# Stick-breaking attention scores: the low part of k held per head in both partition halves, and the second score product run over 128 rows

## The chip, the cores and the metric

The kernel runs on one core of a Trainium2 chip. The metric is the device time of one execution in microseconds (us). The program has five instruction streams: TensorE (PE in the profile; its weight loads are listed apart as PEld), VectorE (DVE), ScalarE (ACT), GpSimd (POOL) and the queue that issues DMAs (SP).

## What is computed

One hybrid decoder layer over x of 1024 tokens by 1024 channels: one input projection; three causal mixers of 256 channels each (stick-breaking attention, HGRN2, GLA); a sigmoid-gated merge of their up-projections; an output projection; residual and layer norm. The change lies in the stick-breaking mixer, which has 4 heads of 64 channels:

```python
z = einsum('bhtd,bhsd->bhts', q, k) * 64 ** -0.5        # per head, s < t
log_beta, log_one_minus = log_sigmoid(z), log_sigmoid(-z)
tail = reverse_cumsum(log_one_minus, over s) - log_one_minus
weights = exp(log_beta + tail)                          # 0 where s >= t
out = einsum('bhts,bhsd->bhtd', weights, v)
```

Inputs and output are float32.

## The kernel before

Matrix products run in a 32-bit matmul type (F32R). To keep accuracy, an operand is split into a high part (a cast) and a low part (the operand minus its cast), and a product is the sum of high·high, low·high and high·low. The helper `split` (lines 97 to 99) does that for weights, for x and for attention weights: the cast is ScalarE's (L98), the subtraction VectorE's (L99).

**Projections.** x^T lies in SBUF in two parts. `proj_T` (L207) makes 128 channels by 512 tokens with 24 matmuls of 512 columns; `proj_N` (L220) makes 128 tokens by 256 or 272 channels with 24 matmuls. They are written as generators that form one stream, in a fixed order: v, then q and k of unit 0, of unit 1, the gates, GLA's inputs, and so on.

**Chains.** The mixers are generators too (`c_sb` for stick-breaking, `c_rec` for the recurrences). The program walks through a chain and, at each `yield`, puts some matmuls of the stream into it, as many as a budget allows. The order on each engine is set when the program is built, by a scheduler that goes by priorities and by which buffers are free; on the chip each engine works through its list in that order.

**Scores.** A unit is two heads, 128 channels. `f_qk` projects k and q of a unit in two halves of 512 tokens. Heads are kept apart by partition half: rA is partitions 0 to 63, rB is 64 to 127. For head 0, `q0` has the high part of q in rA and its low part in rB, and `k0` has the high part of k in both halves; so one product over 128 rows is (high q + low q)·(high k). For head 1 it is the same with the halves changed over (`q1`, `k1`). The low part of k is one tile `l` for both heads: head 0 in rA, head 1 in rB. The second product of a score (L559) therefore takes one half only, 64 rows.

`c_sb` works through 24 chunks per unit, each of 128 queries and up to 512 keys of one head. `weights` makes the score z with two matmuls (L558, L559) into one of two PSUM tiles, two sigmoids on ScalarE (L560, L561), a select on GpSimd where the chunk holds the diagonal (L565), and on VectorE a scan (L569) and a product (L570). Three chunks later `transposed` turns the result with up to four matmuls (L585) and splits it into `ath` (ScalarE, L98) and `atl` (VectorE, L99). One chunk after that `values` multiplies them with v (L607).

**Buffers.** Tiles made by `H` come from one pool of 29 buffers of 128 x 512 x 4 bytes (`NHALF`): 8 of v, the tiles of q and k, the chain's outputs `oT`, and much else.

Of the kernel before, what the change touches and what calls it, by code (L numbers as in the profile page):

```python
# [7 lines left out]
F32 = mybir.dt.float32  # L8
F32R = mybir.dt.float32r
# [3 lines left out]
ALU = mybir.AluOpType  # L13
# [4 lines left out]
T = 1024  # L18
# [37 lines left out]
def hybrid_layer_kernel(ctx, tc, x, x_t, w_in, gla_gate_w2, gla_gate_b, hgrn_lb_logits,  # L56
# [44 lines left out]
    def split3(parts, src):  # L101
        """three parts of bf16 that sum up to src; src is overwritten"""
        nc.scalar.copy(parts[0], src)
        nc.vector.tensor_tensor(src, src, parts[0], op=ALU.subtract)
        nc.scalar.copy(parts[1], src)
        nc.vector.tensor_tensor(parts[2], src, parts[1], op=ALU.subtract)

    def parts3():
        """room for three parts of two halves"""
        a, b, c = [H("prod", BF16, [P, 2, 512]) for _ in range(3)]  # L110
        return [(t[:, 0], t[:, 1], c[:, th]) for th, t in enumerate((a, b))]

    def pairs(pr1, Q, K):
        """products of the odd queries and the keys before them, at the places of these keys"""
        t_ = GT("prod")[:, 0:256]
        nc.vector.tensor_tensor(t_, Q[:, 1::2], K[:, 0::2], op=ALU.mult)
        for p_ in pr1:
            nc.gpsimd.memset(p_[:, 1::2], 0.0)
        split3([p_[:, 0::2] for p_ in pr1], t_)

    class at_priority:
        """trace order within a class; the class of the lower number goes first on an engine"""
        stack, seq = [0], 0
# [18 lines left out]

# [1 line left out]
    wz = const.tile([P, 512], BF16, name="wz")  # L144
# [20 lines left out]

# [1 line left out]
    def load_w(src, c0, width=256, extra=None, between=None):  # L167
        """src [(k p), c], columns c0..c0+width: per k the two parts of the weights [p, width]."""
        nk = src.shape[0] // P
        n = min(nk, 512 // min(width, 256))  # L170
        ks = []
        wt = width if extra is None else width + 16
        for u in range(nk // n):
            raw = wp.tile([P, n, wt], F32, tag="wr", name=nm("wr"), bufs=NWR)
            rows = src[u * n * P:(u + 1) * n * P]
            nc.sync.dma_start(raw[:, :, 0:width], rows[:, c0:c0 + width].rearrange("(k p) c -> p k c", p=P))
            if extra is not None:
                nc.sync.dma_start(raw[:, :, width:wt], rows[:, extra:extra + 16].rearrange("(k p) c -> p k c", p=P))
            wh = wp.tile([P, n, wt], F32R, tag="wh", name=nm("wh"), bufs=5)
            wl = wp.tile([P, n, wt], F32R, tag="wl", name=nm("wl"), bufs=5)  # L180
            with at_priority(PW):
                split(wh, wl, raw)
            ks += [(wh[:, k], wl[:, k]) for k in range(n)]
            if between is not None and u == 1:
                between()
        return ks

# [1 line left out]
    xh = [[xp.tile([P, 4, 512], F32R, tag="x", name=nm("xh")) for _ in range(2)] for _ in range(2)]  # L189
# [10 lines left out]
    def proj_T(ws, th):  # L200
        """generator; the product is what it returns"""
        pt = pmm()
        n = 0
        for k, (wh, wl) in enumerate(ws):
            a, b = xh[th][k // 4][:, k % 4, :], xl[th][k // 4][:, k % 4, :]
            for w_, x_ in ((wh, a), (wh, b), (wl, a)):
                mm(pt, w_, x_, start=(n == 0), stop=(n == 23))  # L207
                n += 1
                if n % 6 == 0 and n < 24:
                    yield 1.3  # L210
        return pt
# [13 lines left out]

# [1 line left out]
    # rows of three products: high high, high low, low high  # L227
    w2 = const.tile([16, P], F32, name="w2")
# [19 lines left out]

    # lower bound of HGRN2: softmax over the depth axis (one layer), cumulated, minus its first row
    lb = const.tile([P, 2], F32, name="lb")  # L250
# [14 lines left out]

    # ======== the stream of projections: generators that yield the time of the tensor engine ========
    def f_av():
# [12 lines left out]
    def f_qk(un):  # L280
        uk = load_w(W, A_K + un * P, P)
        ks, qs, kl = ([], []), ([], []), []
        for th in range(2):
            pt = yield from proj_T(uk, th)
            k0, k1, l = H("ks", F32R), H("ks", F32R), H("kl", F32R)
            nc.scalar.copy(k0[rA], pt[rA])
            nc.scalar.copy(k0[rB], pt[rA])
            nc.scalar.copy(k1[rB], pt[rB])
            nc.scalar.copy(k1[rA], pt[rB])
            nc.vector.tensor_tensor(l[rA], pt[rA], k0.bitcast(F32)[rA], op=ALU.subtract)  # L290
            nc.vector.tensor_tensor(l[rB], pt[rB], k1.bitcast(F32)[rB], op=ALU.subtract)
            ks[0].append(k0)
            ks[1].append(k1)
            kl.append(l)
            yield 1.3
# [35 lines left out]
    def f_cv():  # L331
# [35 lines left out]
        def decay():  # L367
            # f = exp(log_sigmoid(x) / 16), log_sigmoid(x) = min(x, 0) - log(1 + exp(-|x|))
            lower_bound()
# [41 lines left out]
    def f_h(un):  # L411
        uf = load_w(W, H_F + un * P, P)
        f, K, Q = [], [], []
        for th in range(2):
# [3 lines left out]
            nc.scalar.activation(s2, pt, AF.Sigmoid, scale=-1.0)  # L418
            # f = sigmoid(z) (1 + lb exp(min(-z, 60))) = sigmoid(z) + lb min(sigmoid(-z), e^60 sigmoid(z))
            nc.vector.scalar_tensor_tensor(e, s1, E60, s2, op0=ALU.mult, op1=ALU.min)  # L420
# [18 lines left out]
    def f_finish(c0, gain, key, out_key):  # L439
        """gate of a recurrence in natural layout, then y^T."""  # L440
        ws = load_w(W, c0)
# [90 lines left out]

    # ======== chains: generators that yield (time of the chain, share of the tensor engine) ========
    def c_sb(un):
# [11 lines left out]
        def weights(c):  # L546
            """z, beta and 1 - beta, products from the right: the weights of 128 queries and up to 512 keys"""
            hd, jp, g, ti = c
            hr = (rA, rB)[hd]
            i = jp * 2 + ti  # L550
# [7 lines left out]
            mm(pt[:, 0:cm], qq[:, th], ks[hd][g][:, 0:cm], start=True, stop=False)  # L558
            mm(pt[:, 0:cm], qq[hr, th], kl[g][hr, 0:cm], start=False, stop=True)  # L559
            nc.scalar.activation(om[:, 0:cw], pt[:, 0:cw], AF.Sigmoid, scale=-0.125)  # L560
            nc.scalar.activation(be[:, 0:cw], pt[:, 0:cw], AF.Sigmoid, scale=0.125)  # L561
            if last:
                # keys before the query: 1 - beta = 1 and beta = 0 elsewhere
                for a_, fill in ((om, 1.0), (be, 0.0)):
# [11 lines left out]
        def transposed(c):  # L576
# [11 lines left out]
            if ni < ns:  # L588
                # block above the diagonal
                for a_ in (ath, atl):  # L590
                    nc.vector.tensor_scalar(a_[:, ni, ts], ident, 0.0, None, op0=ALU.mult)
# [39 lines left out]
    def c_rec(key, nh, V):  # L631
        """windows of 128; G decay, K key [k, t], Q query; V [t, v]; two halves of t side by side."""
        G, K, Q, pr = d[key]
# [13 lines left out]
        sc = [S("sc", shape=[P, wpb, nh, P]) for _ in range(nbank)]  # L647
        # block-diagonal queries, the odd blocks of a level
        parts = nh == 4
# [3 lines left out]
        if parts:  # L653
            # products of two exact parts; the low parts of the queries by two windows
            Qlo = [[R("Qlo", F32R, [P, nh, P]) for _ in range(2)] for _ in range(2)]
# [50 lines left out]
        for h in LEVELS:  # L706
            nb = 64 // h
            for hf in range(2):
# [11 lines left out]
                yield R4_T if nh == 4 else R2_T  # L720
        # keys in rows of t
        kn = []
# [6 lines left out]
        yield RK_T  # L729
        # states at the starts of windows 1..7, block-diagonal over heads  # L730
        spt = 512 // ncol
# [8 lines left out]
        for b in range(nbank):  # L740
# [13 lines left out]
            yield RS_T / nbank  # L754
        # o = q S + scores v, RMS norm per head
        wpt = 512 // ncol
# [27 lines left out]

    # ======== interleaving: chains first, the stream of projections in their gaps ========
    stream = [("V", f_av()), (("qk", 0), f_qk(0)), (("qk", 1), f_qk(1)), (("ag", 0), f_ag(0)),
# [9 lines left out]
    def advance():  # L796
        """one step of the stream; its time on the tensor engine, or None when it is at its end"""
        while pos[0] < len(stream):
# [53 lines left out]

# [1 line left out]
    wout(range(NWO, 8))  # L854
# [3 lines left out]
    for tq in range(4):  # L858
# [4 lines left out]
        for t2 in range(2):  # L863
# [38 lines left out]
            else:  # L902
                # some of the columns go through ScalarE and GpSimd
                ca, cb, cc = slice(0, 192), slice(192, 640), slice(640, D)
# [41 lines left out]
```

## Time and profile before

| | |
|---|---|
| median of 3 runs | 847.0 us (846.96 to 847.02) |
| the profiled execution: its span, which is also its time | 847.0 us |
| PE busy | 98% of the span, 4576 matmuls |
| PE weight loads busy | 82% |
| DVE busy | 59% |
| ACT busy | 42% |
| POOL busy | 16% |
| DMA, mean over the span | 55 GB/s |
| the first score product starts at | 55.7 us |
| the last score product of `c_sb` starts at | 214.4 us |

"Busy" counts the time in which an engine has an instruction running. Matmuls overlap each other in TensorE's pipeline and their ends are modelled, so 98% does not mean that the engine works at its peak: the distance from the start of one matmul to the start of the next says what a matmul costs. Of an engine other than PE the busy time can be taken as it stands.

### The profile page before, as it was taken

To read this page: it belongs to the slowest core of one execution; us is meant where nothing else is said; L and a number is where in the kernel's file an instruction comes from. 1 tells how busy PE (TensorE), PEld (TensorE's weight loads), DVE (VectorE), ACT (ScalarE), POOL (GpSimd) and SP (SyncE) were. 2 spreads that over 40 slices of the span, in tenths; PEclk is the share of its full clock that TensorE was granted. 3 is DMA by queue.
4 is the path that set the end of the run, shared out by engine and by line. 5 is a ranking of instruction groups with operands and counts; after the bars stand their busy time and mean duration, and the time that the engine had idled before them with its cause. 6 is when DMAs were issued, how large, how long until landed. Compare 5 with 4: busy or idle time off the path is not lost.

```text
span 847.0 us, 12334 instructions
## 1 busy us (share of the span) xinstructions
PE 830.7 (98%) x4576; PEld 697.8 (82%) x4576; DVE 496.7 (59%) x1025; ACT 353.2 (42%) x733; POOL 138.9 (16%) x234
## 2 busy tenths in 40 slices
PE   8999999999999999999999999999999999999996
PEld 7977788777778989988888889888888888878886
DVE  6449886868999868687754124221233223256665
ACT  6457564686634636454655123221222222241110
POOL 3011212022310011422210002222222121110000
PEclk9999999999999999999999999999999999999998
DMA  9421010110011111020412120221212122132211
GB/s 266 108 53 26 26 26 1 45 26 21 24 38 39 40 37 26 2 62 20 126 37 81 38 69 16 54 57 38 57 38 61 32 63 63 44 125 100 95 54 50
DMA packets 66508, 46.22 MB, mean 55 GB/s; under 512 B 4353, under 2 KB 61329, under 8 KB 66449
## 3 DMA queue, kind: packets, MB, share of 16 engines
q1 hardware_dynamic: 65008, 42.36, 18.1%
q10 hardware_dynamic: 1440, 3.08, 1.0%
q8 instruction: 36, 0.59, 0.3%
q14 instruction: 24, 0.19, 0.1%
HBM read 41.23 MB, written 4.19 MB: 54 GB/s over the span
## 4 chain that ended last, share of the span: by engine, by line
PE 88%; DVE 8%; issue 1%; DMA 1%; ACT 0%; POOL 0%; SPq 0%; POOLq 0%; DVEq 0%; ACTq 0%
PE mm L207 43%; PE mm L220 14%; PE mm L878 10%; PE mm L503 7%; PE z L693 4%; PE z L559 2%; PE av L607 2%; PE tr L585 2%; PE av L766 2%; DVE Qlo L677 1%; PE z L558 1%; PE av L764 1%; DVE om L569 1%; DMA wr<-in_w_out_dram 1%; PE z L744 1%
## 5 line engine op out<-in xcount | busy, mean ns | idle before, releaser
L207 PE MATMUL mm<-xh,wh 128*128 128x512 f32 x576 | 233.2, 405 | 0.0
L207 PE MATMUL mm<-xh,wl 128*128 128x512 f32 x576 | 229.2, 398 | 0.0
L207 PE MATMUL mm<-xl,wh 128*128 128x512 f32 x576 | 228.1, 396 | 0.0
L207 PEld LDWEIGHTS mm<-xh,wh 128*128 128x128 f32 x576 | 109.7, 190 | 26.8 <-issue 3.5
L207 PEld LDWEIGHTS mm<-xh,wl 128*128 128x128 f32 x576 | 108.5, 188 | 24.1
L207 PEld LDWEIGHTS mm<-xl,wh 128*128 128x128 f32 x576 | 108.8, 189 | 22.2
L99 DVE TENSOR_TENSOR wl<-wr,wh 128x512 fp32r<-128x512 f32 (+2 forms) x116 | 74.6, 648 | 83.8 <-ACT wh L98 82.8
L98 ACT CAST wh<-wr 128x512 fp32r<-128x512 f32 (+2 forms) x116 | 66.4, 576 | 106.9 <-PE mm L207 92.8
L220 PE MATMUL mm<-wh,xh 128*128 128x256 f32 (+1 forms) x320 | 93.2, 291 | 0.8 <-ACT wh L98 0.8
L220 PE MATMUL mm<-wl,xh 128*128 128x256 f32 (+1 forms) x320 | 91.5, 286 | 0.4 <-DVE wl L99 0.4
L220 PE MATMUL mm<-wh,xl 128*128 128x256 f32 (+1 forms) x320 | 91.0, 285 | 0.0
L878 PE MATMUL mm<-wo,mh 128*128 128x512 f32 (+1 forms) x288 | 80.8, 366 | 0.3 <-DVE wo L99 0.3
L509 POOL TENSOR_TENSOR mT<-mT,gt 128x512 f32<-128x512 f32 x32 | 46.8, 1462 | 179.3 <-DVE gt L508 179.3
L508 DVE TENSOR_TENSOR gt<-mm,gt 128x512 f32<-128x512 f32 x32 | 22.1, 690 | 83.3 <-PE mm L503 83.0
L497 ACT ACTIVATE gt<-mm 128x512 f32<-128x512 f32 x48 | 28.6, 595 | 97.8 <-PE mm L207 91.8
L220 PEld LDWEIGHTS mm<-wh,xh 128*128 128x128 f32 x320 | 61.0, 191 | 2.9 <-ACT wh L98 1.7
L220 PEld LDWEIGHTS mm<-wl,xh 128*128 128x128 f32 x320 | 61.0, 190 | 1.1 <-DVE wl L99 1.1
L220 PEld LDWEIGHTS mm<-wh,xl 128*128 128x128 f32 x320 | 61.0, 191 | 0.1
L878 PEld LDWEIGHTS mm<-wo,mh 128*128 128x128 f32 x288 | 52.0, 189 | 9.5 <-DVE wo L99 0.7
L878 PE MATMUL mm<-wo,ml 128*128 128x512 f32 (+1 forms) x144 | 52.6, 365 | 0.0
L503 PE MATMUL mm<-yl,wh 128*128 128x512 f32 x96 | 38.5, 401 | 1.9 <-DVE yl L99 1.9
L503 PE MATMUL mm<-yh,wl 128*128 128x512 f32 x96 | 38.4, 399 | 0.0
(204 smaller groups left out, 1290.8 us busy)
## 6 DMA issues: line engine op xcount, KB each, us to landing
wr<-in_w_in_dram SPq DMA_DIRECT2D x92, 256.0 KB, 2.9
xraw<-in_x_t_dram SPq DMA_DIRECT2D x16, 256.0 KB, 5.5
xr<-in_x_dram SPq DMA_DIRECT2D x8, 512.0 KB, 3.4
wr<-in_w_out_dram SPq DMA_DIRECT2D x16, 256.0 KB, 2.8
wr<-in_w_up_dram SPq DMA_DIRECT2D x24, 128.0 KB, 2.3
out_dram<-xr SPq DMA_DIRECT2D x7, 256.0 KB, 2.1
out_dram<-xr ACTq DMA_DIRECT2D x7, 256.0 KB, 2.1
lng<-in_ln_g_dram ACTq DMA_DIRECT2D x1, 512.0 KB, 4.8
```

The costliest lines, as they stand in the source:

```text
L98: nc.scalar.copy(hi, src)
L99: nc.vector.tensor_tensor(lo, src, hi.bitcast(F32), op=ALU.subtract)
L207: mm(pt, w_, x_, start=(n == 0), stop=(n == 23))
L220: mm(pt, x_, w_, start=(n == 0), stop=(n == 23))
L497: nc.scalar.activation(gt, pt, AF.Sigmoid)
L503: mm(pu, w_, y_[th], start=(k == 0), stop=(k == 5))
L508: nc.vector.tensor_tensor(gt, pu, gt, op=ALU.mult)
L509: nc.gpsimd.tensor_tensor(mT, mT, gt, op=ALU.add)
L559: mm(pt[:, 0:cm], qq[hr, th], kl[g][hr, 0:cm], start=False, stop=True)
L585: nc.tensor.transpose(pt[:, j, :], be[:, j * P:(j + 1) * P], ident)
L693: mm(pt[:, wi * nh:(wi + 1) * nh], k_[:, w * P:(w + 1) * P], q.rearrange("p a (n h) -> p a n h", h=h), start=(n == 0 and wi == 0), stop=(n ...
L878: mm(pt, l_, r_[e][:, o:o + w], start=(n == 0), stop=(n == 23))
```

## The change

The low part of k is kept per head, each in both partition halves, as the high part is. The second product is then (high q + low q)·(low k) over 128 rows, with the same stationary operand as the first product. It adds the product of the two low parts, which was left out before.

```diff
     def f_qk(un):
         uk = load_w(W, A_K + un * P, P)
-        ks, qs, kl = ([], []), ([], []), []
+        ks, qs, kl = ([], []), ([], []), ([], [])
         for th in range(2):
             pt = yield from proj_T(uk, th)
-            k0, k1, l = H("ks", F32R), H("ks", F32R), H("kl", F32R)
+            k0, k1, l0, l1 = H("ks", F32R), H("ks", F32R), H("kl", F32R), H("kl", F32R)
...
-            nc.vector.tensor_tensor(l[rA], pt[rA], k0.bitcast(F32)[rA], op=ALU.subtract)
-            nc.vector.tensor_tensor(l[rB], pt[rB], k1.bitcast(F32)[rB], op=ALU.subtract)
+            for r_ in (rA, rB):
+                nc.vector.tensor_tensor(l0[r_], pt[rA], k0.bitcast(F32)[rA], op=ALU.subtract)
+                nc.vector.tensor_tensor(l1[r_], pt[rB], k1.bitcast(F32)[rB], op=ALU.subtract)
             ks[0].append(k0)
             ks[1].append(k1)
-            kl.append(l)
+            kl[0].append(l0)
+            kl[1].append(l1)
...
         def weights(c):
             hd, jp, g, ti = c
-            hr = (rA, rB)[hd]
...
             mm(pt[:, 0:cm], qq[:, th], ks[hd][g][:, 0:cm], start=True, stop=False)
-            mm(pt[:, 0:cm], qq[hr, th], kl[g][hr, 0:cm], start=False, stop=True)
+            mm(pt[:, 0:cm], qq[:, th], kl[hd][g][:, 0:cm], start=False, stop=True)
```

Per unit it makes four subtractions more on VectorE and two `H` tiles more. The rest of the diff takes out comments. Line numbers behind the change are up by one or two.

The built order of the instructions moves in a few places while `c_sb` of unit 0 runs. On VectorE, at the first half of unit 1's k: before, the two subtractions L290 and L291 (`kl`) stand ahead of the split of the chain (`atl`) and its scan (`om`).

```order
L591 TENSOR_SCALAR atl_724<-ident 128x128
L290 TENSOR_TENSOR kl_716<-mm_635,ks_714 64x512
L291 TENSOR_TENSOR kl_716<-mm_635,ks_715 64x512
L99 TENSOR_TENSOR atl_724<-tr_725,ath_723 128x128
L569 SCALAR_TENSOR_TENSOR om_739<-om_739 128x128
L99 TENSOR_TENSOR wl_1079<-wr_1076,wh_1078 128x512
L570 TENSOR_TENSOR be_738<-be_738,om_739 128x127
L99 TENSOR_TENSOR atl_724<-tr_751,ath_723 128x2x128
```

With the change (lines 291 and 292):

```order
L592 TENSOR_SCALAR atl_733<-ident 128x128
L291 TENSOR_TENSOR kl_722<-mm_641,ks_720 64x512
L292 TENSOR_TENSOR kl_723<-mm_641,ks_721 64x512
L291 TENSOR_TENSOR kl_722<-mm_641,ks_720 64x512
L99 TENSOR_TENSOR wl_1091<-wr_1088,wh_1090 128x512
L292 TENSOR_TENSOR kl_723<-mm_641,ks_721 64x512
L99 TENSOR_TENSOR atl_733<-tr_734,ath_732 128x128
L570 SCALAR_TENSOR_TENSOR om_748<-om_748 128x128
L99 TENSOR_TENSOR atl_733<-tr_760,ath_732 128x2x128
L571 TENSOR_TENSOR be_747<-be_747,om_748 128x127
```

Four subtractions and the split of a weight (`wl`) now stand ahead of the chain's `atl` and scan. On TensorE some 50 rows of the same stretch are in another order. Before, a chunk's three transposes (`tr_777`) and all products with v (`av_791`) stand ahead of the score z_801:

```order
L585 MATMUL tr_777<-ident,be_682 128x128 x3
L207 MATMUL mm_731<-xh_115,wl_632 128x512
L207 MATMUL mm_731<-xh_115,wh_631 128x512
L207 MATMUL mm_731<-xl_119,wh_631 128x512
L207 MATMUL mm_731<-xh_115,wl_632 128x512
L607 MATMUL av_791<-ath_723,V_205 128x256
L607 MATMUL av_791<-atl_724,V_205 128x256
L607 MATMUL av_791<-ath_723,V_205 128x256
L607 MATMUL av_791<-atl_724,V_205 128x256
L558 MATMUL z_801<-ks_506,qs_617 128x512
L559 MATMUL z_801<-kl_508,qs_617 128x512
```

With the change (the same tiles are tr_786, av_800 and z_810):

```order
L608 MATMUL av_800<-ath_732,V_205 128x256
L559 MATMUL z_810<-ks_506,qs_623 128x512
L560 MATMUL z_810<-kl_508,qs_623 128x512
L207 MATMUL mm_740<-xh_115,wh_637 128x512
L207 MATMUL mm_740<-xl_119,wh_637 128x512
L586 MATMUL tr_786<-ident,be_688 128x128 x3
L207 MATMUL mm_740<-xh_115,wl_638 128x512
L608 MATMUL av_800<-atl_733,V_205 128x256
L608 MATMUL av_800<-ath_732,V_205 128x256
L608 MATMUL av_800<-atl_733,V_205 128x256
```

The transposes and three of the four products with v now stand behind the score and two projection matmuls. By the end of unit 0's first head the two orders agree again on TensorE, and from there on they are the same to the end of the program. ScalarE's list differs in two places by one position; the DMA queue's list is the same.

## Rows read from the trace of the kernel before

**Rows 1.** The page's first part: the span, and the engines' busy time.
```profile
span 847.0 us, 12334 instructions
PE 830.7 (98%) x4576; PEld 697.8 (82%) x4576; DVE 496.7 (59%) x1025; ACT 353.2 (42%) x733; POOL 138.9 (16%) x234
```
**Rows 2.** The chain of work that ended last, by engine.
```profile
PE 88%; DVE 8%; issue 1%; DMA 1%; ACT 0%; POOL 0%; SPq 0%; POOLq 0%; DVEq 0%; ACTq 0%
```
**Rows 3.** Busy time by stretch: length, PE, PEld, DVE, ACT, POOL, clock, DMA.
```profile
50.00:60.00 10.00, 10.00 (x43) 7.46 (x41) 5.16 (x9) 5.37 (x10) 1.11 (x4) 1.00 0.23 56
60.00:90.00 30.00, 29.39 (x137) 21.49 (x137) 26.77 (x50) 21.42 (x46) 5.68 (x12) 1.00 0.08 19
90.00:130.00 40.00, 40.00 (x234) 32.44 (x234) 34.52 (x68) 21.97 (x50) 7.28 (x16) 1.00 0.10 27
130.00:200.00 70.00, 69.33 (x391) 55.50 (x391) 52.56 (x110) 47.21 (x98) 15.74 (x35) 1.00 0.11 27
200.00:220.00 20.00, 19.92 (x100) 14.92 (x99) 19.79 (x36) 13.48 (x30) 2.93 (x8) 1.00 0.10 27
```
**Rows 4.** The same stretches, the 64-row product (L559) alone: PE, PEld.
```profile
50.00:60.00 10.00, 0.77 (x2) 0.36 (x2) 1.00 0.23 56
60.00:90.00 30.00, 5.01 (x11) 2.01 (x11) 1.00 0.08 19
90.00:130.00 40.00, 5.00 (x11) 2.01 (x11) 1.00 0.10 27
130.00:200.00 70.00, 8.31 (x19) 3.47 (x19) 1.00 0.11 27
200.00:220.00 20.00, 2.41 (x5) 0.91 (x5) 1.00 0.10 27
```
**Rows 5.** TensorE in order of time, 512 columns: start us, duration us, instruction.
```profile
82.10 0.39 PE L558 MATMUL z<-ks,qs 128*128 128x512 f32 x1
82.42 0.49 PE L559 MATMUL z<-kl,qs 64*128 64x512 f32 x1
82.84 0.50 PE L207 MATMUL mm<-xh,wh 128*128 128x512 f32 x1
83.18 0.39 PE L207 MATMUL mm<-xl,wh 128*128 128x512 f32 x1
83.41 0.40 PE L207 MATMUL mm<-xh,wl 128*128 128x512 f32 x1
```
**Rows 6.** The weight loads of the same stretch; in brackets idle time before.
```profile
82.42 0.18 PEld L559 LDWEIGHTS z<-kl,qs 64*128 64x128 f32 x1 [0.25 <-issue]
82.84 0.19 PEld L207 LDWEIGHTS mm<-xh,wh 128*128 128x128 f32 x1 [0.24 <-issue]
82.95 0.19 PEld L207 LDWEIGHTS mm<-xl,wh 128*128 128x128 f32 x1
```
**Rows 7.** TensorE in order of time, a score of 256 columns among proj_N's matmuls.
```profile
144.10 0.28 PE L558 MATMUL z<-ks,qs 128*128 128x256 f32 x1
...
144.85 0.29 PE L220 MATMUL mm<-wh,xl 128*128 128x272 f32 x1
144.98 0.29 PE L220 MATMUL mm<-wl,xh 128*128 128x272 f32 x1
```
**Rows 8.** Who waited for whom, 50 to 215 us: total us, times, longest.
```profile
DVE om L569 <- POOL om L565: 10.3, 16, 1.6
PEld z L559 <- issue: 9.9, 39, 0.4
```
**Rows 9.** VectorE's L301, from one partition half to the other: ns min/median/max.
```profile
L301 DVE TENSOR_TENSOR qs<-mm,qs x4: 683/684/684, 49.5 to 94.4; 64x512 fp32r<-64x512 f32 x4
```
**Rows 10.** TensorE in order of time: a product with v that waits for VectorE.
```profile
88.25 0.39 PE L607 MATMUL av<-atl,V 128*128 128x256 f32 x1 [0.61 <-DVE atl L99]
```
**Rows 11.** TensorE in order of time: the last score that reads unit 0's second key half, head 0.
```profile
79.32 0.50 PE L559 MATMUL z<-kl,qs 64*128 64x512 f32 x1
```
**Rows 12.** ScalarE in order of time: a cast into a q tile of unit 1.
```profile
84.68 0.58 ACT L302 CAST qs<-mm 64x512 fp32r<-64x512 f32 x1 [0.59 <-DVE qs L301]
```

## The prediction

> **What bounds the kernel now.** I begin with the page's busy times: TensorE has something running in 98% of the span [rows 1], and the chain of work that ended last lies on it for 88%, on VectorE for 8% [rows 2]. So time taken off TensorE counts, unless VectorE becomes the later one. The change sits in a piece of the program from 50 to 215 us, so next I read the busy times by stretch. There the reader is to see the VectorE column: 26.8 of 30 us from 60 to 90, 34.5 of 40 up to 130, 52.6 of 70 up to 200, and 19.8 of 20 from 200 to 220 [rows 3]. TensorE leads and VectorE is close behind it, in the last stretch level with it.
>
> Last I read TensorE's start times around one score. Two projection matmuls of 512 columns start 0.23 us apart (83.18 to 83.41) [rows 5]. From the first score product (82.10) to the second matmul behind the pair (83.18) there are three distances, which at 0.23 would be 0.69 us; they take 1.08 [rows 5]. The weight loads show why: the 64-row load begins only at 82.42, with its own matmul, after 0.25 us in which nothing loaded; the 128-row load behind it also begins with its matmul, after another 0.24 us [rows 6]. An ordinary load begins earlier, beneath the matmul before it: the one at 82.95 belongs to the matmul at 83.18 [rows 5, 6]. So **each 64-row product costs twice: once on going to 64 rows and once on going back**. The list of waits says the same from its side: before the 64-row load the loader sat idle 39 times, 9.9 us in all, and waited for no other engine ("issue") [rows 8].
>
> **The change, part by part.**
>
> *The 64-row product becomes a 128-row one.* The excess of a pair is 1.08 - 0.69 = 0.39 us with 512 columns. With 256 columns, among proj_N's matmuls, three distances take 0.75 us (144.10 to 144.85), where the ordinary one is 0.13, so 0.39: excess 0.36 [rows 7]. I take 0.38. There are 48 such pairs: 2, 11, 11, 19 and 5 in the five stretches [rows 4]. If TensorE alone set the time, 48 x 0.38 = 18.2 us would go. The new product streams as many columns as the old one, and 128 rows against 64 add no columns, so I cost the product itself at nothing: the first product of the pair has that shape now. From below the row bound is zero gain (the pause belongs to this second product whatever its rows), from above 18.2; I take the full price for the pair because both pauses stand exactly at the two places where the row count changes, and no 128-row neighbour in these rows has one.
>
> A page of the Trainium skill speaks against this: TensorE: Matmul & The Clock Gate, Part 3, "The mechanism", says that a weight load overlaps matmuls in flight only when its group of rows differs. By that the new 128-row load, behind a 128-row matmul, would wait as well, and the sum would hold no saving at all. The trace disagrees: the load at 82.95 runs under a 128-row matmul that started at 82.84 and takes 0.50 us [rows 5, 6].
>
> *Eight subtractions more on VectorE.* Two of them move data from one partition half to the other, as L301 does now; that one takes 0.68 us [rows 9]. I take 0.69 for each: 5.5 us. Half of them (unit 0's k, 2.8 us) come before 50 us, when no chain runs yet; there I cost them at nothing, since the scores start only behind the projections of q. If that cover is gone they cost 2.8. The other half (unit 1's k, 2.8 us) falls into 60 to 90 us, ahead of the chain's split and scan in VectorE's queue, as the built order shows. Who waits for that: the transposes and the products with v. One of these already waits 0.61 us for VectorE, at 88.25 [rows 10].
>
> *TensorE's order in that stretch.* The transposes and products with v stand later, behind the next score, so TensorE goes past a late VectorE more easily. No instruction is added by that; I cost it at nothing, and use it only as a reason not to count VectorE's load twice.
>
> *Two tiles more per unit in the pool of 29.* While unit 0's first head runs, the pool would hold 8 tiles of v, up to 12 of unit 0, outputs and up to 10 of unit 1, about as many as there are. A cast into a q tile of unit 1 starts at 84.68 [rows 12]; the last score that reads two of unit 0's tiles starts at 79.32 and takes 0.50 [rows 11]. That is a margin of some 4.9 us, so I cost it at nothing. DMA issues are the same in number and order.
>
> *The sum, by stretch, with the later of the two engines* [rows 3, 4].
> - 50 to 60: 2 x 0.38 = 0.8 us; VectorE is half idle. 0.8.
> - 60 to 130: 22 x 0.38 = 8.4 us on TensorE. VectorE has 26.77 + 34.52 + 2.76 = 64.05 us of work in 70, so no more than 5.95 can go. It would then have no gap at all, yet it now waits 10.3 us in all for GpSimd's selects [rows 8], which come between ScalarE and its scans. I take half: 3.0.
> - 130 to 200: 19 x 0.38 = 7.2 us; VectorE would have 52.6 in 62.8. TensorE is idle 0.7 us there, which shows that other waits exist; I take that off: 6.5.
> - 200 to 220: 5 x 0.38 = 1.9 us, but VectorE's work is 19.79 of 20: 0.2.
>
> Together 10.5 us. Behind 220 us the order is unchanged and everything only starts earlier. The profiled execution took 847.0 us, the same as the median of the runs, so 847.0 - 10.5 = **836.5 us**.
>
> **The rivals.**
>
> *TensorE alone sets the time.* VectorE's late results do not matter, because a chunk's transposes come three chunks later and the new order puts some later still. For it: TensorE idles only 0.61 us in 60 to 90 although VectorE is 89% busy [rows 3]. Against it: products with v follow the split by one chunk, and 200 to 220 is full. It gives 847.0 - 18.2 = 828.8, or up to 832.8 with VectorE just full (0.8 + 5.95 + 7.2 + 0.2 = 14.2). Chance 0.13.
>
> *VectorE eats most of it.* Nothing is left in 60 to 130, and only half in 130 to 200: 0.8 + 0 + 3.6 + 0 = 4.4, so 842.6; I give this case 840 to 845.3. For it: the wait of rows 10, and selects, scans and splits that follow each other without much room. Against it: 52.6 of 70 us from 130 to 200. Chance 0.12.
>
> *No change.* The pause belongs to the second product, not to its 64 rows, for instance because a load can't overtake a matmul that uses the same rows. Then the pair stays as long as it is and the four subtractions in 60 to 90 hide in VectorE's 3.2 idle us: 847, within 0.2%. That is the skill's rule from the mechanism section named above. The load at 82.95 and every ordinary one speak against it. Chance 0.07.
>
> *Slower.* TensorE saves less than VectorE adds. Place: VectorE's queue from 65 to 76 us, where four more subtractions stand ahead of split and scan; price 2.8 us, or 5.5 if unit 0's four delay the first score too: 849.8 to 852.5. It decides the result once the saving on TensorE is under 2.8 us, which takes a pair's saving of under 0.06 us. Chance 0.04.
>
> **How the numbers follow.** My forecast has 0.64. A difference of under 0.2% (1.7 us) can't be told from no change here. Faster by more: 0.64 + 0.13 + 0.12 = 0.89; within it: 0.07; slower: 0.04. The range 830.5 to 842.5 leaves out a part of the first rival (0.04), of the second (0.04), and the last two (0.11): 0.19. It takes in the bounds of the uncertain stretch, 60 to 130 us (0 to 5.95 around my 3.0), and of 130 to 200 (3.6 to 7.2).
>
> **What would show it right or wrong.** Right: the wait of the L559 load on "issue" is gone (now L560); the three distances around a score take some 0.70 us with 512 columns; second products have 128 rows and the duration of the first ones; VectorE is over 95% busy from 60 to 125 us; the last score of the second unit starts some 10 us before 214. A saving of over 14 us would say that VectorE's fill does not hold TensorE up; new waits of transposes or products with v on VectorE, several us in all, with a saving under 7, would say that it does so more than I think. If the load of the second product still begins only with its matmul, my reading of the pause is wrong.

## The result, and the profile after

The changed kernel takes **838.25 us** (median of 4 runs, 837.8 to 838.5), the kernel before in the same comparison 847.01 (846.96 to 847.12). The ratio is 0.9895, interval 0.9883 to 0.9906: faster by 8.8 us.

The page of the changed kernel, its first part and its chain by engine; they answer to [rows 1] and [rows 2]:

```profile
span 836.3 us, 12346 instructions
PE 813.9 (97%) x4576; PEld 694.8 (83%) x4576; DVE 500.6 (60%) x1033; ACT 352.0 (42%) x733; POOL 138.2 (17%) x234
...
PE 80%; DVE 11%; issue 4%; ACT 2%; POOL 1%; DMA 1%; SPq 0%; POOLq 0%; DVEq 0%; ACTq 0%
```

TensorE's busy time falls by 16.8 us (830.7 to 813.9), almost twice what the time falls by, and the chain shows where the rest stayed: VectorE 8% before, 11% now. So TensorE does the same work in less time, and waits more.

The spans of the two profiled executions are not compared directly. In the one of before the first projection began at 32.0 us, in the one of after at 30.8, ahead of all that the change touches; from 8 to 12 us TensorE's mean granted clock is 0.58 in the first and 1.00 in the second. The span of the changed kernel is also 1.9 us less than the time of the same execution (836.3 of 838.19), and the runs below show 1.8 to 2.1. So the span of 847.0 us before, which was taken to be the time of that execution too, suggests one that was about 1.9 us slower than the median; the forecast starts from the median and is not touched by it. I compare from score to score instead. These are the second products of the 1st, 3rd, 25th, 44th and 48th score, from TensorE's timeline, of before and then of after. 2, 22, 19 and 4 pairs lie between them, so they stand for the four stretches of the prediction (the last of which had five).

```profile
55.91 0.38 PE L559 MATMUL z<-kl,qs 64*128 64x256 f32 x1
...
60.02 0.44 PE L559 MATMUL z<-kl,qs 64*128 64x384 f32 x1
...
134.60 0.38 PE L559 MATMUL z<-kl,qs 64*128 64x256 f32 x1
...
202.97 0.49 PE L559 MATMUL z<-kl,qs 64*128 64x512 f32 x1
...
214.41 0.49 PE L559 MATMUL z<-kl,qs 64*128 64x512 f32 x1
```
```profile
54.65 0.28 PE L560 MATMUL z<-kl,qs 128*128 128x256 f32 x1
...
57.96 0.34 PE L560 MATMUL z<-kl,qs 128*128 128x384 f32 x1
...
129.24 0.28 PE L560 MATMUL z<-kl,qs 128*128 128x256 f32 x1
...
191.99 0.39 PE L560 MATMUL z<-kl,qs 128*128 128x512 f32 x1
...
204.08 0.39 PE L560 MATMUL z<-kl,qs 128*128 128x512 f32 x1
```

Each difference of two starts before, minus the same after, is what that stretch saved:

| scores | before | after | saved | predicted |
|---|---|---|---|---|
| 1 to 3 | 4.11 | 3.31 | 0.80 | 0.8 |
| 3 to 25 | 74.58 | 71.28 | 3.30 | 3.0 |
| 25 to 44 | 68.37 | 62.75 | 5.62 | 6.5 |
| 44 to 48 | 11.44 | 12.09 | -0.65 | 0.2 |
| together | 158.50 | 149.43 | 9.07 | 10.5 |

One clean score, from TensorE's timeline of after, 512 columns; beside it its weight loads:

```profile
82.23 0.47 PE L559 MATMUL z<-ks,qs 128*128 128x512 f32 x1
82.55 0.39 PE L560 MATMUL z<-kl,qs 128*128 128x512 f32 x1
82.77 0.39 PE L207 MATMUL mm<-xh,wh 128*128 128x512 f32 x1
83.00 0.39 PE L207 MATMUL mm<-xl,wh 128*128 128x512 f32 x1
```
```profile
82.20 0.19 PEld L559 LDWEIGHTS z<-ks,qs 128*128 128x128 f32 x1
82.31 0.19 PEld L560 LDWEIGHTS z<-kl,qs 128*128 128x128 f32 x1
82.55 0.19 PEld L207 LDWEIGHTS mm<-xh,wh 128*128 128x128 f32 x1
```

Against [rows 5] and [rows 6]: the three distances take 0.77 us instead of 1.08, and 0.32 of that is the first one, whose weights had begun to load only at 82.20. The load of the second product starts at 82.31, only 0.11 us after the load before it and beneath a matmul that runs from 82.23, where before it started with its own matmul and 0.25 us of idle ahead of it. Both loads and both matmuls use the same 128 rows, so what the Trainium skill says in TensorE: Matmul & The Clock Gate, Part 3, "The mechanism" (a load overlaps only when its group of rows differs) is not what this trace shows. The same section of the Trainium skill also lets a load into the background weight buffer go ahead of matmuls in flight. Whether this load is of that kind, no row here shows.

Busy time by stretch (columns as in [rows 3]; the last line is the stretch of the forecast's sign on VectorE), and TensorE's, its loader's and VectorE's largest waits in the same region:

```profile
50.00:60.00 10.00, 10.00 (x47) 8.18 (x46) 5.58 (x10) 6.46 (x13) 2.14 (x7) 1.00 0.23 56
60.00:90.00 30.00, 27.25 (x143) 21.68 (x142) 29.21 (x53) 19.98 (x45) 5.25 (x12) 1.00 0.11 28
90.00:130.00 40.00, 39.18 (x264) 35.66 (x263) 35.07 (x72) 23.06 (x53) 5.99 (x14) 1.00 0.08 21
130.00:200.00 70.00, 68.17 (x404) 58.46 (x402) 59.45 (x123) 51.54 (x109) 16.48 (x39) 1.00 0.11 27
200.00:220.00 20.00, 17.83 (x139) 14.40 (x138) 19.91 (x38) 12.38 (x27) 5.48 (x9) 1.00 0.10 27
60.00:125.00 65.00, 61.55 (x366) 52.59 (x364) 62.25 (x119) 41.25 (x93) 11.25 (x26) 1.00 0.10 26
```
```profile
DVE om L570 <- POOL om L566: 5.3, 10, 1.3
PE av L608 <- DVE atl L99: 3.8, 5, 1.5
PE tr L586 <- DVE atl L99: 1.3, 2, 1.0
...
PE tr L353 <- DVE atl L99: 0.7, 1, 0.7
...
PE tr L363 <- DVE atl L99: 0.2, 1, 0.2
```

TensorE now idles 7.6 us of the 170, where before it idled 1.4: 6.2 more. 6.0 us of idle time ends with one thing, VectorE's split of the transposed weights into their high and low part (atl, L99): the products with v need the low part, and the transposes need the buffer that the split empties. The loader's wait on "issue" of 9.9 us [rows 8] is gone; no row of the second product's load has it any more.

### The profile page after: what moved, and what is told of

It reads as the page before. It is cut to its first block, busy times and chain, and to the rows that moved or that the text cites. A ratio compares the mean times of both kernels' runs of the same rounds, so it can differ in the third digit from the quotient of the medians.

```text
span 836.3 us, 12346 instructions
## 1 busy us (share of the span) xinstructions
PE 813.9 (97%) x4576; PEld 694.8 (83%) x4576; DVE 500.6 (60%) x1033; ACT 352.0 (42%) x733; POOL 138.2 (17%) x234
## 3 DMA queue, kind: packets, MB, share of 16 engines
q1 hardware_dynamic: 65008, 42.36, 18.2%
## 4 chain that ended last, share of the span: by engine, by line
PE 80%; DVE 11%; issue 4%; ACT 2%; POOL 1%; DMA 1%; SPq 0%; POOLq 0%; DVEq 0%; ACTq 0%
PE mm L207 40%; PE mm L220 12%; PE mm L879 11%; PE mm L505 7%; PE z L694 4%; DVE om L570 2%; PE av L767 2%; DVE atl L99 1%; PE av L608 1%; DVE Qlo L678 1%; DVE be L571 1%; PE av L765 1%; DVE wl L99 1%; PE z L745 1%; DMA xraw<-in_x_t_dram 1%
## 5 line engine op out<-in xcount | busy, mean ns | idle before, releaser
L207 PE MATMUL mm<-xh,wh 128*128 128x512 f32 x576 | 230.3, 400 | 0.0
L99 DVE TENSOR_TENSOR wl<-wr,wh 128x512 fp32r<-128x512 f32 (+2 forms) x116 | 74.5, 649 | 80.6 <-ACT wh L98 79.4
L566 POOL TENSOR_SCALAR_AFFINE_SELECT om<-om 128x128 f32<-128x128 f32 x32 | 13.3, 414 | 151.3 <-ACT om L561 146.8
```

Source lines behind the costliest of these rows:

```text
L99: nc.vector.tensor_tensor(lo, src, hi.bitcast(F32), op=ALU.subtract)
```

## The experiments

**Is it the 64 rows, or the second product whatever its rows?** My theory: the row count. The rival: a product behind another into the same sum pauses with any shape. The first run keeps the changed kernel, its order and its subtractions, and multiplies over 64 rows again.

```
-  mm(pt[:, 0:cm], qq[:, th], kl[hd][g][:, 0:cm], ...)
+  mm(pt[:, 0:cm], qq[(rA, rB)[hd], th], kl[hd][g][(rA, rB)[hd], 0:cm], ...)
```

> The changed kernel, with the second product taken back to the 64 rows of its own head; the eight subtractions more, the tiles and the order of all instructions stay as in the change. It leaves out the product of the two low parts, as the kernel before does. Theory (the pause belongs to the change of the row count): the pauses are back, about 0.38 us a pair, and with them the time: 847 to 849 us, that is the kernel before plus 0 to 2 us for VectorE's extra work in 60 to 90 us. The load of the second product again waits on 'issue' some 40 times, 9 to 10 us in all. Rival (the gain comes from the new order of the instructions, or from the tiles, and not from the rows): about 838 us, as the change.

Measured 848.04 us, ratio to before 1.0007 (0.9999 to 1.0016). The loader's list of waits has the old row back:

```profile
PEld z L560 <- issue: 9.7, 38, 0.4
```

All 9.8 us that separate this run from the changed kernel go with the number of rows. What else the change did (subtractions, tiles, order) costs at most the 0.8 us by which this run lies above the kernel before (847.25 beside it), as long as TensorE is the slower engine.

This run and the changed kernel have the same 844 matmuls in the same order between the first and the last second product of a score, so their timelines can be laid side by side, distance by distance. The two ends in the run with 64 rows (in the changed kernel they are 54.65 and 204.08, above):

```profile
54.98 0.38 PE L560 MATMUL z<-kl,qs 64*128 64x256 f32 x1
...
214.30 0.50 PE L560 MATMUL z<-kl,qs 64*128 64x512 f32 x1
```

Between them the changed kernel is 9.9 us shorter. At the 47 pairs its distances are shorter by 17.6 us, 0.37 a pair. Elsewhere they are longer by 7.6: 5.7 of that ahead of matmuls that VectorE's split released, 1.1 ahead of such that ScalarE released, and 0.8 where the profile names no engine. So nearly the whole price shows at the pairs, and what takes a part of it back is mostly the wait for the split.

**The converse: the wide product without the subtractions**, in the kernel before and in its order; the low part of q then also meets the other head's low part of k.

```
-  mm(pt[:, 0:cm], qq[hr, th], kl[g][hr, 0:cm], start=False, stop=True)
+  mm(pt[:, 0:cm], qq[:, th], kl[g][:, 0:cm], start=False, stop=True)
```

> The kernel before, with the second product over all 128 rows of the one low tile, in which the two heads lie in different halves: the scores take in a wrong share of the other head. No subtraction, no tile and no change of order. It is what TensorE alone gives. Theory (rows cost switches, and VectorE's extra 2.8 us in 60 to 90 us hold part of the gain back): 1 to 3 us faster than the change, 835.5 to 837.5 us. Rival A (VectorE's extra work costs nothing): as the change, 838.2. Rival B (VectorE does not hold TensorE up at all): about 829 us. Rival C (the new order is what helps): slower than 840.

Measured 836.47 us, ratio 0.9873 (0.9859 to 0.9886): 10.8 us gained, 2.0 more than the change itself (8.8). In its timeline a score that comes out of no wait has the distances that I had forecast:

```profile
78.63 0.40 PE L558 MATMUL z<-ks,qs 128*128 128x512 f32 x1
78.86 0.40 PE L559 MATMUL z<-kl,qs 128*128 128x512 f32 x1
79.10 0.39 PE L207 MATMUL mm<-xh,wh 128*128 128x512 f32 x1
79.33 0.39 PE L207 MATMUL mm<-xl,wh 128*128 128x512 f32 x1
```

Three distances, 0.70 us in all. Yet 48 pairs at 0.38 would be 18.2, and even without the subtractions 10.8 came.

**Few rows, or a change of rows?** Both products of the pair over 64 rows (the low part of q against the high part of k is left out).

```
-  mm(pt[:, 0:cm], qq[:, th], ks[hd][g][:, 0:cm], start=True, stop=False)
+  mm(pt[:, 0:cm], qq[hr, th], ks[hd][g][hr, 0:cm], start=True, stop=False)
```

> The kernel before, with the first product of a score also over the 64 rows of its head; it leaves out the product of the low part of q with the high part of k. Now two 64-row products follow each other, and there are still two changes of the row count a pair. Theory (the change costs, not the 64 rows): the second 64-row load starts beneath the first product and its wait on 'issue' moves to the first product's load; time as before, 846 to 848 us. Rival (each 64-row product costs a pause of its own): 48 more products with a pause, up to 18 us on TensorE, 853 to 865 us.

Measured 846.6 us, ratio 0.9991 (0.9982 to 1.0). The weight loads around one score:

```profile
83.50 0.18 PEld L558 LDWEIGHTS z<-ks,qs 64*128 64x128 f32 x1 [0.17 <-issue]
83.61 0.19 PEld L559 LDWEIGHTS z<-kl,qs 64*128 64x128 f32 x1
84.17 0.19 PEld L207 LDWEIGHTS mm<-xh,wh 128*128 128x128 f32 x1 [0.37 <-issue]
```

The pause has moved, not grown. The second 64-row load follows the first after 0.11 us, beneath the first product; the idle time now stands ahead of the first 64-row load and ahead of the load that goes back to 128 rows. So the price belongs to the change of row count, in both directions, and not to 64 rows as such.

**What do the subtractions cost?** Without the four of each unit that carry over to the other half: those halves are filled with zeros on GpSimd, which leaves out the product of the two low parts.

```
+  nc.gpsimd.memset(l0.bitcast(F32)[rB], 0.0)
+  nc.gpsimd.memset(l1.bitcast(F32)[rA], 0.0)
-  for r_ in (rA, rB):
-      nc.vector.tensor_tensor(l0[r_], ...)
-      nc.vector.tensor_tensor(l1[r_], ...)
+  nc.vector.tensor_tensor(l0[rA], ...)
+  nc.vector.tensor_tensor(l1[rB], ...)
```

> The changed kernel, but the low part of k is subtracted in its own half only, as before, and the other half is filled with zeros by GpSimd: eight 64-row fills in place of eight subtractions. The second product is over 128 rows and computes what the kernel before computed. Theory (VectorE is full from 60 to 100 us and holds TensorE up there): 1 to 3 us faster than the change, 835.5 to 837.5 us, and near the run that has 128 rows in the kernel before. Rival (VectorE's subtractions are hidden): 838.2 us. Second rival (the fills delay GpSimd's selects, for which the scans wait): 838.5 to 840 us.

Measured 836.65 us, ratio 0.9876 (0.9863 to 0.989): 1.6 us below the changed kernel, close to the run with the wide product alone (1.8 below it). The other way round, unit 1's subtractions made twice, eight more of 0.69 us, 5.5 us of VectorE:

```
-  for r_ in (rA, rB):
+  for r_ in (rA, rB) * (1 + un):
```

> The changed kernel, with the eight subtractions of unit 1 made twice over (eight more, 0.69 us each, 5.5 us of VectorE between 60 and 90 us); the result is the same. Theory (VectorE is the bound from 60 to 100 us): the time grows by most of it, 3 to 5.5 us over the change, 841 to 844 us. By the two runs before this one, four subtractions in that stretch cost 0.8 us with the pauses and 1.8 us without them. Rival (TensorE goes past a late VectorE): within 1 us of the change, 838 to 839.

Measured 841.87 us, ratio 0.9943 (0.9929 to 0.9957): 3.6 us above the changed kernel, 0.65 of what was added to VectorE. Between the 3rd and the 25th score, where unit 1's four subtractions stand, the run with zeros takes 69.62 us against 71.28: 1.66 of the 2.76 us taken out, 0.60; the run with the subtractions twice takes 75.3 there, 4.0 of the 5.5 us put in, 0.73. So VectorE's work there counts for six to seven tenths.

**Does VectorE hold back the rest?** If so, more should come through once VectorE has less to do. First both kernels without the product be*om (L571 and L573 after, L570 and L572 before), a full-width operation of each chunk on VectorE beside scan and split.

```
-  nc.vector.tensor_tensor(be[:, 0:cw - 1], be[:, 0:cw - 1], om[:, 1:cw], op=ALU.mult)
-  if not last:
-      nc.vector.tensor_tensor(be[:, cw - 1:cw], be[:, cw - 1:cw], rt[:, 0:1], op=ALU.mult)
```

> The changed kernel without the product of beta with the running product of 1 - beta (the line behind the scan and its one-column follower): the attention weights are left as bare betas. It takes 0.3 to 0.7 us per chunk, about 28 us in all, off VectorE, and the transposes no longer wait for the scan. It is to be read against the next kernel alone. Theory (of the 18.2 us on TensorE, VectorE's fill took back what did not show): with VectorE out of the way the whole price shows, 15 to 18.5 us between the two. Rival (something else, such as ScalarE or the score's two PSUM tiles, takes it back): 9 to 12 us, as with VectorE full.

> The kernel before without the same product (it leaves out the same part). Theory: TensorE was the bound up to 200 us, so little goes: 841 to 846 us, most of it from 200 to 220 us where VectorE was full. Rival (VectorE was already the bound in much of the stretch): below 838 us.

Measured 830.53 us (ratio 0.9804, 0.9792 to 0.9817) with the change and 843.16 (0.9951, 0.9938 to 0.9964) without it. The change is worth 12.6 us between them instead of 8.8: more comes through, but neither my 15 to 18.5 nor the rival's 9 to 12. In the first of the two TensorE still waits for the split:

```profile
PEld av L605 <- DVE atl L99: 3.7, 6, 1.2
...
PE av L605 <- DVE atl L99: 2.0, 4, 1.0
```

So the split itself was taken out as well: no low part of the weights, no products with it, no be*om, once with the second product over 64 rows and once over 128.

```
-  split(ath[:, 0:ni, ts], atl[:, 0:ni, ts], pt[:, 0:ni, :])
+  nc.scalar.copy(ath[:, 0:ni, ts], pt[:, 0:ni, :])
...
-  for n, a_ in enumerate(at_):
+  for n, a_ in enumerate(at_[:1]):
```

> The kernel before without the product of beta with the running product, and without the low parts of the attention weights (their split's subtraction and their products with v): what TensorE does between score and output no longer waits for VectorE. To be read against the next kernel alone. 830 to 842 us, since 80 matmuls of 256 columns (about 0.12 us each, 9.6 us) and some of VectorE's work from 200 us on are gone.

> The kernel of the run before this one, with the second score product over all 128 rows of the one low tile, as in the second experiment; every engine has the same instructions in the same order. Theory (a pair's pauses cost 0.38 us, 18.2 us for 48 pairs, and only VectorE's late splits hid a part of it in the runs so far): 16.5 to 18.5 us less than the run before this one. Rival (the pauses were overstated by the start times, and 11 to 13 us is all that there is): 10.5 to 13.5 us less.

Measured 835.22 us (ratio 0.9864, 0.9847 to 0.988) and 820.9 (0.9686, 0.9667 to 0.9705). The 14.3 us between them again lie between the two expectations, but here the trace tells the rest. TensorE has the same matmuls in the same order in both. These are the second products of the 1st and the 36th score and the first of the 40th, first in the run with 64 rows, then in the one with 128, there with the three matmuls behind it:

```profile
55.00 0.38 PE L559 MATMUL z<-kl,qs 64*128 64x256 f32 x1
...
156.04 0.49 PE L559 MATMUL z<-kl,qs 64*128 64x512 f32 x1
...
175.99 0.50 PE L558 MATMUL z<-ks,qs 128*128 128x512 f32 x1 [2.30 <-ACT be L561]
```
```profile
54.94 0.28 PE L559 MATMUL z<-kl,qs 128*128 128x256 f32 x1
...
143.06 0.39 PE L559 MATMUL z<-kl,qs 128*128 128x512 f32 x1
...
162.65 0.80 PE L558 MATMUL z<-ks,qs 128*128 128x512 f32 x1 [2.80 <-ACT be L561]
163.24 0.63 PE L559 MATMUL z<-kl,qs 128*128 128x512 f32 x1
163.67 0.63 PE L207 MATMUL mm<-xl,wh 128*128 128x512 f32 x1
164.10 0.63 PE L207 MATMUL mm<-xh,wl 128*128 128x512 f32 x1
```

From the 1st to the 36th score TensorE idles in neither run, and 12.92 us (101.04 less 88.12) are gained over 35 pairs, **0.369 us a pair**; 48 of them are **17.7**. Ahead of the 40th score both wait for ScalarE, and the 128-row run goes on with its matmuls 0.43 us apart. Some of the gain is lost there for a reason that is told further down.

**Can VectorE be relieved, or the order loosened?** Three variants of the kernel with zeros. The first takes the low parts of the weights of several projections to GpSimd:

```
-  split(wh, wl, raw)
+  nc.scalar.copy(wh, raw)
+  nc.gpsimd.tensor_tensor(wl, raw, wh.bitcast(F32), op=ALU.subtract)
```

> The kernel with zero-filled halves (836.65 us), and the low parts of the weights of q, k, the attention gates, and GLA's v, k and q are subtracted by GpSimd: some 19 of VectorE's operations, about 13 us, leave it between 50 and 220 us. GpSimd takes about twice as long for one (its product of 512 columns takes 1.46 us against 0.69). Theory (VectorE's fill is what is left to gain): 2 to 6 us faster, 831 to 835 us. Rival (GpSimd's selects, for which the scans wait, come later by its new work, or the weights come late): 836 to 842 us.

Measured 840.05 us, ratio 0.9922 (0.9909 to 0.9935), 3.4 slower than with the zeros alone. VectorE waits 8.9 us for GpSimd's selects instead of 5.3, and one transpose waits 3.1 us for a split:

```profile
DVE om L575 <- POOL om L571: 8.9, 12, 1.5
...
PEld tr L358 <- DVE atl L99: 3.1, 1, 3.1
```

The selects stand in GpSimd's queue behind the subtractions, 1.4 us each there (13 of them). The second variant makes the products with v one chunk later:

```
-  values(chunks[k - SB_LAG - 1])
+  values(chunks[k - SB_LAG - 2])
```

> The kernel with zero-filled halves (836.65 us), in which a chunk's products with v come two chunks behind its transposes instead of one, so that TensorE meets a late split less often. Theory (the wait of products with v for VectorE's split is what took back the gain): 2 to 5 us faster, 831.5 to 835 us. Rival (VectorE is full and the wait only moves to another place): 836 to 837.5 us; with two more tiles in use at a time it can also be slower.

Measured 837.25 us, ratio 0.9885 (0.987 to 0.99): nothing gained. The wait goes to the next one in line, the transposes that need the split's buffer, and to a score behind ScalarE:

```profile
PEld tr L587 <- DVE atl L99: 5.5, 6, 1.9
PEld z L560 <- ACT be L563: 3.2, 1, 3.2
```

Behind that last wait TensorE's mean granted clock is 0.83 from 170 to 180 us, and the four executions go from 835.98 us at a mean clock of 0.997 to 839.09 at 0.992. So a part of this kernel's time goes with the clock; even the fastest of them lies only 0.7 below the median with zeros alone.

The third fills the blocks above the diagonal on GpSimd:

```
-  nc.vector.tensor_scalar(a_[:, ni, ts], ident, 0.0, None, op0=ALU.mult)
+  nc.gpsimd.memset(a_.bitcast(F32)[:, ni, ts], 0.0)
```

> The kernel with zero-filled halves (836.65 us), in which GpSimd instead of VectorE clears the blocks above the diagonal: 32 of VectorE's operations at 0.22 us, 7 us in all, leave it. Theory (VectorE's fill is what is left): 1 to 3 us faster, 833.5 to 835.5 us. Rival (GpSimd's selects come later by it, as with the weights' low parts): 836.5 to 839 us.

Measured 835.92 us, ratio 0.9871 (0.9856 to 0.9886): 0.7 below the kernel with zeros, with intervals that overlap, so it can't be told from it. Three variants end near 836.5 and beat both kernels; they do without the product of the two low parts, as the kernel before does, or put another head's in its place.

## Why the prediction was right

The forecast was 836.5 us, the result is 838.25, inside the range and 1.7 us slow of it. By its steps:

- **The pair price.** Right in its mechanism: putting 64 rows back takes the whole gain away, and a run with two 64-row products shows the pause at the places where the row count changes. It is right in size too: it was read from two scores of before as 0.38 us, and the two comparisons of equal sequences of matmuls give 0.369 and 0.374, so 17.7 to 18.0 us for 48 pairs where 18.2 was forecast.
- **The product itself at nothing.** It now lasts as long as the first (0.28 us with 256 columns, 0.39 with 512), and the distances are the ordinary ones.
- **The eight subtractions.** They last 0.69 us as said. Unit 0's are hidden: the first score starts 23.8 us behind the first projection with them and without them (54.65 less 30.8, 54.47 less 30.6). Unit 1's are not: the wide product without them saved 5.33 us from the 3rd to the 25th score, with them 3.30. So 2.0 of their 2.8 us reach the end there, and 1.6 to 2.0 are seen in the runs. They are in the sum, as VectorE's 2.76 us of work.
- **50 to 60, 60 to 130.** 0.80 and 3.30 measured, 0.8 and 3.0 forecast. The sign was right: VectorE is busy 62.25 of the 65 us from 60 to 125, 96%. Taking half of VectorE's room was a choice between two ends, and that it came within 0.3 us is luck as much as reading: its reason, the waits for GpSimd's selects, held up in part (10.3 us [rows 8], now 5.3). Against the run with 64 rows the pairs from the 3rd to the 25th score give 8.4 us, as forecast, and 4.2 of that is lost, 3.2 of it ahead of matmuls that the split released.
- **130 to 200.** 6.5 forecast, 5.62 measured. The pairs give 7.0 of the 7.2 us of that step; the rest of the miss is waiting, which was costed too low: TensorE idles 1.8 us of the 70, and I had taken off the 0.7 that it idled before.
- **200 to 220.** 0.2 forecast, -0.65 measured. VectorE is full there, as before, but TensorE now comes to it earlier and idles 2.2 us of the 20, where it idled 0.1: four pairs give 1.4 us, and waits take 2.0, 1.6 of it for the split. I had counted on the full engine to give next to nothing; it also took back a little that had been gained earlier. This step and the one before fall short by 0.85 and 0.88 us, the stretch from 60 to 130 brought 0.30 more than forecast, and 0.3 lies outside the scores: that is the miss of 1.7.
- **Order, tiles in the pool, DMA at nothing.** The run with 64 rows in the changed kernel has all three and lies 0.8 us above the kernel before, not to be told from it.

So 17.7 us of price become 10.8 because of the work that VectorE already has, and 8.8 because of the subtractions. The sum closes from score to score: 17.6 at the pairs less 7.6 behind waits is the 9.9 us to the run with 64 rows (0.1 is in small shifts), and that run is 0.8 us longer there than the kernel before, which leaves 9.1; the table has 9.07. TensorE's idle time rises by only 6.2 us, because it counts from the modelled end of a matmul, 0.16 us behind the point at which the next could start (0.39 us long, 0.23 apart with 512 columns).

Of the rivals, "TensorE alone" failed on VectorE's split: it holds TensorE up for 6.0 us. "VectorE eats most" overrated it; half of the price arrives. "No change" fell with the weight loads, and "slower" needed a pair price under 0.06 us. That VectorE is what holds the rest back is shown by more coming through when it has less to do: 8.8 us as it is, 12.6 without one of its products, 14.3 without that and the split. The last figure is cut short by the clock, as told below.

## What to carry to other kernels

Look in the weight loader's waits for idle time that waits for no engine, and ask whether the matmul behind it uses another number of rows than its neighbours: a product over few rows between others over all rows costs twice, once each way, and here was cheaper padded with zeros. That it can stand beside others of its own row count at no extra cost is what the run with both products over 64 rows shows. Price what that frees on TensorE, then ask stretch by stretch what share the next engine lets through; here it was 8.8 of 17.7 us, and each microsecond put on that engine where it is full cost six to seven tenths of itself. Compare two traces from landmark to landmark, since a stretch that is full on the second engine can also give back what was gained ahead of it.

## What the runs showed of the hardware

A change between 64 and 128 rows on TensorE costs time both ways, 0.37 us for the two together, and a 64-row load behind another 64-row product costs nothing extra (83.50 to 83.61 in the run with both products over 64 rows). The Trainium skill has the rule in TensorEngine Tiling (Array Packing), "Key Properties": a change of the tiling mode drains TensorE. It gives no price; the trace agrees with the rule if 64 of 128 rows count as another mode.

Less expected was the clock. In the 128-row run without VectorE's work TensorE waited 2.80 us for ScalarE, and behind that its matmuls of 512 columns started 0.43 us apart (163.24 to 163.67) instead of 0.23. The busy times by stretch of that run show the granted clock in the column behind POOL's:

```profile
160.00:170.00 10.00, 7.35 (x20) 5.82 (x21) 6.06 (x10) 7.16 (x13) 6.08 (x9) 0.66 0.24 55
...
200.00:205.00 5.00, 5.00 (x47) 4.23 (x46) 3.94 (x6) 3.92 (x9) 2.80 (x2) 0.50 0.00 0
```

A mean of 0.66 in the first and 0.50 in the second: the lower of the clock's two levels, 1.2 GHz, for part of the one and all of the other. Ahead of the second TensorE had idled 1.6 us of 20. In the run with 64 rows a wait of 2.30 us came at the same place and the mean was 0.83 there. In the changed kernel the granted clock stays at 1.00 in all five stretches, its 7.6 us of idle time notwithstanding. A TensorE that is made faster until it waits can lose some of what it won in this way. The four executions of the 128-row kernel give the size: three with a mean granted clock of 0.990 or 0.991 took 820.87 to 822.25 us, the one with 0.998 took 818.04. That is 17.2 us below the median of the kernel with 64 rows, which points to the clock for most of the missing 3.4 us (17.7 less 14.3). It is not shown outright: it is a single execution, and those of the kernel with 64 rows, at 0.994 and 0.995, have some of the low clock too.
